# The context's second pointwise product of a convolution module in plain fp32, from unsplit maps and weights, with a third slot for raw weights

## The chip, the cores and the metric

The kernel runs on one NeuronCore of a Trainium2 chip, as one program. The metric is the device time of one execution in microseconds (us), smaller is better. It has five engines that are programmed apart and meet through semaphores: TensorE (PE, matrix products, with its weight loads shown as PEld), VectorE (DVE), ScalarE (ACT), GpSimd (POOL) and SyncE (SP, which here only issues transfers).

## The reference, cut to what matters

A backbone of two layers works on 1024 latent tokens and a context of 256 tokens, with 1024 features, all in fp32. Layer 0 is a Conformer convolution module, layer 1 grouped-query attention; a SwiGLU feed-forward follows each. The change lies in layer 0, in the two lines behind the convolution, for the context's tokens alone:

```python
def layernorm(x, g, b):
    mu = jnp.mean(xf, axis=-1, keepdims=True)
    var = jnp.mean(jnp.square(xf - mu), axis=-1, keepdims=True)
    y = (xf - mu) * lax.rsqrt(var + EPS)
    return (y * g + b)

def conv_module(h, w_pw1, b_pw1, w_dw, b_dw, ln_g, ln_b, w_pw2, b_pw2):
    u = h @ w_pw1 + b_pw1
    a, gt = jnp.split(u, 2, axis=-1)
    u = a * jax.nn.sigmoid(gt)
    u = lax.conv_general_dilated(u, w_dw, ...) + b_dw
    u = jax.nn.silu(layernorm(u, ln_g, ln_b))
    return u @ w_pw2 + b_pw2
```

Both streams, latent and context, go through it with the same weights.

## The kernel before, in words

Features lie on the 128 partitions, in 8 groups (KT), tokens along the free dimension. The tokens come in three pieces: C (the context, 256 tokens), L and R (the two halves of the latent tokens, 512 each).

**Products.** A large fp32 product is made of three fp32r products. An operand x is split into hi, its rounding to fp32r (a cast on ACT), and lo = x - hi (a subtraction on DVE); then hi\*hi, hi\*lo and lo\*hi are added up in one PSUM bank (`mm3`, L165 to L167; `mm3s`, L176 to L178, does the same for several weights at once, interleaved). `wload` (L135) brings a weight of 128x1024: SP loads it into a raw slot (tile `wr`, L141), ACT casts it (L142), DVE subtracts (L146). There are two raw slots and three buffers each for the halves (`wh`, `wl`). Weights that were loaded ahead wait in the list `self.pre`. Small products (sums over partitions with a column of ones, L363, transposes, L375, and the layer norm's mean, L562) take their operands in plain fp32, unsplit.

**The stage.** After the convolution, whose last maps DVE builds (L500) while PE uses them (L526 to L529), each piece goes through `ln` and `pw2`. `ln`: the mean over features (`mean`, L556: one fp32 product per phase of the tokens, 8 for C, 4 for L and for R, from the sums `vsum` that DVE made in the convolution); 8 times subtract it (DVE, L580), square (ACT), add up (DVE, L387); the sums of squares to a reciprocal root (`stat`: L363 on PE, small DVE steps L368 and L329 to L337, transposes L375 on PE); 8 times multiply (DVE, L588), Silu (ACT, L590) and split into the two halves (ACT L154, DVE L157). `pw2`: for each of 8 output groups a weight, 24 products (L603), bias and copy to SBUF (ACT, L604), square (ACT) and add (DVE, L387).

**The order of the work.** The program is written piece by piece: `ln` of C and of L, `pw2` of C, `ln` of R, `pw2` of L, post-norm of C and L, `pw2` of R, then the feed-forward. A scheduler in the framework reorders this by priority and data before it is fixed, so that on each engine the instructions of several pieces interleave; in the run each engine takes its own list strictly in order. So the mean of L and the mean of R stand on PE inside the products of C. A mean takes a PSUM bank of the pair 5 and 6 ("st"), which the transposed statistic of the piece before also uses and DVE reads in L588.

The names of tiles: `KB` holds C's convolution output and later its result, `T1` C's two halves, `T4` and `T2`, `T3` belong to L, `T5` and `T6`, `HS` to R; `q` is a room of 128x1024 that holds the convolution's split taps until the last maps are built; `HR` holds `vsum`; `vc` and `vl` are scratch in DRAM through which the convolution's output changes its layout.

Of the kernel before, what the change touches and what calls it, by code (L numbers as in the profile page):

```python
# [11 lines left out]
AF = mybir.ActivationFunctionType  # L12
ALU = mybir.AluOpType
AX = mybir.AxisListType

P = 128
D = 1024
KT = D // P
CTX = 256
# [17 lines left out]
PH = 8  # L37
# [17 lines left out]
class Kern:  # L55
# [79 lines left out]
    def wload(self, ap):  # L135
        nc = self.nc
        n = int(np.prod(ap.shape[1:]))
        raw = self.raw()[:, :n]
        hi = self.wp.tile([P, 1024], F32R, tag="wh", name="wh")[:, :n]
        lo = self.wp.tile([P, 1024], F32R, tag="wl", name="wl")[:, :n]  # L140
        nc.sync.dma_start(raw if len(ap.shape) == 2 else raw.rearrange("p (a b) -> p a b", a=ap.shape[1]), ap)  # L141
        nc.scalar.copy(hi, raw)  # L142
        self.share += self.lo_dve
        if self.share >= 1:
            self.share -= 1
            nc.vector.tensor_tensor(lo, raw, hi.bitcast(F32), op=ALU.subtract)  # L146
        else:
            nc.gpsimd.tensor_tensor(lo, raw, hi.bitcast(F32), op=ALU.subtract)
        return hi, lo

    def split(self, hi, lo, src, hi_eng="act"):
        nc = self.nc
# [403 lines left out]
    def mean(self, b):  # L556

        nc = self.nc
        ps = self.bank("st")
        nn, o, s0 = {"C": (NC_, 0, 0), "L": (NL, 2 + NC_, 0), "R": (NL, 2 + NC_, 4)}[b]  # L560
        for i in range(PH if b == "C" else 4):
            nc.tensor.matmul(ps[:, i * nn:(i + 1) * nn], lhsT=self.c["selp"][:, s0 + i:s0 + i + 1].to_broadcast([P, P]),  # L562
                             rhs=self.vsum[:, o:o + nn], start=True, stop=True)
        return ps
# [6 lines left out]
    def ln(self, b, stags, box):  # L571

        nc, c = self.nc, self.c
        c0, c1 = PIECES[b]
        n = c1 - c0
        cv = self.cvs[b]
        mean = self.mean(b)[:, :n]
        acc = self.acc(n)
        for k in range(KT):
            nc.vector.tensor_tensor(cv[:, k, :], cv[:, k, :], mean, op=ALU.subtract)  # L580
            self.sq_acc(acc, cv[:, k, :], k)
            yield
        pb = self.stat(acc, n)
        shi, slo = self.halves(*stags, n)
        box.append((shi, slo))
        for k in range(KT):
            z = cv[:, k, :]
            nc.vector.scalar_tensor_tensor(out=z, in0=z, scalar=c["lng"][:, k:k + 1], in1=pb,  # L588
                                           op0=ALU.mult, op1=ALU.mult)
            nc.scalar.activation(z, z, AF.Silu, bias=c["lnb"][:, k:k + 1], scale=1.0)  # L590
            self.split(shi[:, k, :], slo[:, k, :], z)
            yield

    def pw2(self, b, ytag, s, box):
# [4 lines left out]
        yacc = self.acc(n)  # L599
        box.append((y, yacc))  # L600
        for k in range(KT):
            o = self.bank("mm")
            self.proj(o, self.a["pw2"][k], self.pairs(*s), n)  # L603
            nc.scalar.activation(y[:, k, :], o[:, :n], AF.Identity, bias=c["bpw2"][:, k:k + 1], scale=1.0)  # L604
            self.sq_acc(yacc, y[:, k, :], k)
            yield 24 * n / 2400
# [338 lines left out]
    def build(self):  # L945
# [92 lines left out]
            self.split_u(KT - 1, g0, g0 + CG // 2)  # L1038
        self.derive(0, (1, 2))
        for i, _ in enumerate(cg):  # L1040
            if i in (2, 4):
                self.pre.append(self.wload(a["pw2"][i // 2 - 1]))
        self.set_banks(mm=[0, 1, 2, 3, 4, 7], st=[5, 6])
        sv, yv, fv = ({b: [] for b in PIECES} for _ in range(3))
        tags = {"C": ("KB", ("T1", "T1"), ("T1", "T1")), "L": ("T4", ("T2", "T3"), ("T2", "T3")),
# [11 lines left out]
            pass  # L1057
        for _ in self.pw2("L", tags["L"][0], sv["L"][0], yv["L"]):
            pass
        for b in ("C", "L"):  # L1060
            for _ in pp(b):
                pass
# [270 lines left out]
```

## Time and profile before

| | |
|---|---|
| Time, median of 3 runs | 3055.4 us (3049.22 to 3057.86) |
| Time of the profiled execution | 3058.17 us, 2.8 above that median |
| Span of the profiled execution, first to last instruction | 3056.4 us |
| Mean granted clock of TensorE | 0.974 |
| PE busy | 2927.2 us (96%) |
| DVE busy | 1902.2 us (62%) |
| ACT busy | 1207.4 us (40%) |

The profile is one execution, recorded instruction by instruction. In a row of the timeline stand the start in us, the duration (of a row with several instructions: of all of them), the engine, the line of the kernel, the operation, what it writes and reads, the shape and how many; in brackets how long the engine had been idle before, and what ended that. Records of matmuls overlap, since they are pipelined: what one costs is read from the distance of starts. The clock is the share of full speed granted to TensorE.

### The profile page before, as it was taken

The page shows a single profiled execution, that of the slowest core. Times are in us where ns is not written, and L with a number is a line of the kernel's source. Part 1 is how long each engine was busy: PE and PEld are TensorE (multiplying, and loading weights), DVE is VectorE, ACT ScalarE, POOL GpSimd, SP SyncE. Part 2 cuts the span into 40 slices and gives each one's busy share as a digit, 9 for nine tenths or more (in the row PEclk, how much of TensorE's full clock was granted, in tenths as well). Part 3 has the DMA queues.
Part 4 walks back from the last instruction along what each step waited for, and adds up shares of the span by engine and source line. Part 5 has one row for each costly group of instructions (what it writes and reads, how often), then busy time and mean ns, then how long its engine had stood idle before and what let it go on. Part 6 is the DMA issues. An engine that isn't in the chain of part 4 may idle for free. (4 is left out here: it accounts for less than half of the span.)

```text
span 3056.4 us, 39302 instructions
## 1 busy us (share of the span) xinstructions
PE 2927.2 (96%) x15086; PEld 2438.8 (80%) x15086; DVE 1902.2 (62%) x3341; ACT 1207.4 (40%) x1981; POOL 261.1 (9%) x413
## 2 busy tenths in 40 slices
PE   7899969999999999999988999999999999999997
PEld 5788868888888888888877777777787778788886
DVE  5886777866566358333565899766666654743335
ACT  5222255432222234222333688645555542332222
POOL 0000000101112011000013111110000000100000
PEclk9999979999999999999989999989999999999999
DMA  6542424433346235333346311223223132443332
GB/s 236 147 122 75 122 76 138 159 114 126 119 156 198 67 105 157 105 97 97 126 134 151 88 45 47 92 70 90 72 69 86 58 135 95 148 136 97 97 93 66
DMA packets 140716, 336.96 MB, mean 110 GB/s; under 512 B 39920, under 2 KB 61424, under 8 KB 139376
## 3 DMA queue, kind: packets, MB, share of 16 engines
q1 hardware_dynamic: 76432, 221.94, 22.6%
q0 software_dynamic: 37984, 104.42, 11.5%
q10 hardware_dynamic: 26112, 8.10, 1.1%
q8 instruction: 118, 1.93, 0.3%
q14 instruction: 70, 0.57, 0.1%
HBM read 289.76 MB, written 39.19 MB: 108 GB/s over the span
## 5 line engine op out<-in xcount | busy, mean ns | idle before, releaser
L167 PE MATMUL ps<-T,wl 128*128 128x512 f32 (+1 forms) x2128 | 802.9, 378 | 11.8 <-DVE wl L146 11.8
L165 PE MATMUL ps<-T,wh 128*128 128x512 f32 (+1 forms) x2128 | 806.3, 380 | 6.9 <-ACT T L154 4.1
L166 PE MATMUL ps<-T,wh 128*128 128x512 f32 (+1 forms) x2064 | 777.9, 377 | 0.7 <-DVE T L157 0.7
L142 ACT CAST wh<-wr 128x1024 fp32r<-128x1024 f32 x296 | 310.8, 1050 | 796.8 <-PE ps L166 569.0
L146 DVE TENSOR_TENSOR wl<-wr,wh 128x1024 fp32r<-128x1024 f32 x288 | 352.0, 1223 | 311.5 <-ACT wh L142 307.1
L167 PEld LDWEIGHTS ps<-T,wl 128*128 128x128 f32 x2128 | 407.3, 192 | 85.9 <-DVE wl L146 14.1
L165 PEld LDWEIGHTS ps<-T,wh 128*128 128x128 f32 x2128 | 407.2, 192 | 79.7 <-ACT T L154 5.6
L166 PEld LDWEIGHTS ps<-T,wh 128*128 128x128 f32 x2064 | 395.5, 192 | 68.9 <-DVE T L157 2.0
L166 PE MATMUL ps<-HS,wh 128*128 128x512 f32 (+1 forms) x784 | 303.8, 388 | 0.0
L892 DVE TENSOR_TENSOR T<-ps,T 128x512 fp32r<-128x512 f32 x320 | 216.7, 686 | 110.9 <-ACT T L891 109.7
L167 PE MATMUL ps<-HS,wl 128*128 128x512 f32 (+1 forms) x720 | 278.9, 388 | 0.0
L165 PE MATMUL ps<-HS,wh 128*128 128x512 f32 (+1 forms) x720 | 278.7, 389 | 0.0
L891 ACT CAST T<-ps 128x512 fp32r<-128x512 f32 x320 | 185.9, 585 | 194.8 <-PE ps L888 172.8
L888 PE MATMUL ps<-cst,T 128*128 128x128 f32 x1100 | 192.2, 276 | 1.9 <-DVE T L892 1.8
L876 DVE TENSOR_SCALAR_CACHE_REDUCE T<-ps,rq 128x1280 f32<-128x1280 f32 x110 | 169.9, 1544 | 27.8 <-PE ps L870 23.0
L722 DVE TENSOR_TENSOR T<-ps,T 128x512 f32<-128x512 f32 (+1 forms) x168 | 110.3, 662 | 113.1 <-PE ps L167 112.2
L888 PEld LDWEIGHTS ps<-cst,T 128*128 128x128 f32 x1100 | 134.0, 142 | 49.0 <-DVE T L892 28.6
L878 ACT ACTIVATE T<-T,mn 128x1280 f32<-128x1280 f32 x110 | 150.4, 1367 | 57.1 <-DVE T L876 55.2
L166 PEld LDWEIGHTS ps<-HS,wh 128*128 128x128 f32 x784 | 147.5, 188 | 28.6 <-DVE HS L157 0.2
L697 DVE TENSOR_TENSOR sm<-sm,ps 128x256 f32<-128x256 f32 (+1 forms) x88 | 54.5, 619 | 181.4 <-PE ps L167 181.2
L870 PE MATMUL ps<-KB,q 128*128 128x512 f32 (+1 forms) x576 | 146.8, 374 | 14.2 <-DVE HS L876 9.9
L167 PEld LDWEIGHTS ps<-HS,wl 128*128 128x128 f32 x720 | 135.4, 188 | 27.0
(227 smaller groups left out, 4574.0 us busy)
## 6 DMA issues: line engine op xcount, KB each, us to landing
wr<-in_w SPq DMA_DIRECT2D x220, 512.0 KB, 3.5
q<-in_w SPq DMA_DIRECT2D x44, 512.0 KB, 3.5
wr<-in_pw SPq DMA_DIRECT2D x40, 512.0 KB, 3.6
HR<-in_wmodT POOLq DMA_DIRECT2D x56, 256.0 KB, 3.9
q<-in_wmodT POOLq DMA_DIRECT2D x56, 256.0 KB, 3.9
qsd<-T POOLq DMA_DIRECT2D x32, 256.0 KB, 10.7
q<-qsd POOLq DMA_DIRECT2D x32, 256.0 KB, 3.3
wr<-in_wo SPq DMA_DIRECT2D x16, 512.0 KB, 4.4
```

What stands on the lines that cost most here:

```text
L142: nc.scalar.copy(hi, raw)
L146: nc.vector.tensor_tensor(lo, raw, hi.bitcast(F32), op=ALU.subtract)
L165: nc.tensor.matmul(out[:, :n], lhsT=wh, rhs=xh, start=k == 0, stop=False)
L166: nc.tensor.matmul(out[:, :n], lhsT=wh, rhs=xl, start=False, stop=False)
L167: nc.tensor.matmul(out[:, :n], lhsT=wl, rhs=xh, start=False, stop=k == nk - 1)
L722: nc.vector.tensor_tensor(yd, out[:, :c1 - c0], yd, op=ALU.add)
L870: nc.tensor.matmul(sc[:, k0:k0 + w], lhsT=q[:, h, :], rhs=kt[:, p * TOK + k0:p * TOK + k0 + w], start=p == 0, stop=p == 1)
L876: nc.vector.tensor_scalar(out=pt, in0=sc, scalar1=rq[:, h:h + 1], scalar2=None, op0=ALU.mult, op1=ALU.min, accum_out=mn)
L878: nc.scalar.activation(pt, pt, AF.Exp, bias=mn, scale=-1.0, accum_out=sums[:, 0, h:h + 1])
L888: nc.tensor.transpose(tp[:, h * P:(h + 1) * P], Ps[h][:, j * P:(j + 1) * P], c["ident"])
L891: nc.scalar.copy(ph, tp)
L892: nc.vector.tensor_tensor(pl, tp, ph.bitcast(F32), op=ALU.subtract)
```

## The change

For the context, and for it alone, `pw2` multiplies plain fp32 operands: 64 products of 128x256 (8 outputs by 8 groups) in the place of 192 fp32r products.

- `ln` of C writes Silu's result straight into one fp32 tile in `T1`; the 8 casts and 8 subtractions of its operand are gone.
- `pw2` of C takes its weights as they are loaded (`load_raw`), with no cast and no subtraction. A slot is free again when the 8 products that read it are done. The three weights that were loaded and split during the convolution are two now, and raw.
- From the eighth step of the last convolution loop on, the room `q` is a third raw slot, until `pw2` of L is written.
- `pw2` of L and of R take their first two weights as an interleaved pair (`projs`).
- The mean of C is one product of 256 columns with a matrix of ones; DVE first spreads `vsum` over the phases with one multiplication (L568 of the new kernel, the product is L570).

```diff
+    def load_raw(self, ap):
+        raw = self.raw()
+        self.nc.sync.dma_start(raw, ap)
+        return raw
...
-        nn, o, s0 = {"C": (NC_, 0, 0), "L": (NL, 2 + NC_, 0), "R": (NL, 2 + NC_, 4)}[b]
-        for i in range(PH if b == "C" else 4):
+        if b == "C":
+            m = self.sm(CTX)
+            mv, shape = m.rearrange("p (s n) -> p s n", n=NC_), [P, PH, NC_]
+            nc.vector.tensor_tensor(mv, self.vsum[:, :NC_].unsqueeze(1).to_broadcast(shape),
+                                    self.c["selp"].unsqueeze(2).to_broadcast(shape), op=ALU.mult)
+            nc.tensor.matmul(ps[:, :CTX], lhsT=self.c["ones"].to_broadcast([P, P]), rhs=m, start=True, stop=True)
+            return ps
+        nn, o, s0 = {"L": (NL, 2 + NC_, 0), "R": (NL, 2 + NC_, 4)}[b]
+        for i in range(4):
...
-        shi, slo = self.halves(*stags, n)
-        box.append((shi, slo))
+        if b == "C":
+            s = self.T(stags[0], [P, KT, n])
+            box.append(s)
+        else:
+            shi, slo = self.halves(*stags, n)
+            box.append((shi, slo))
...
+            if b == "C":
+                nc.scalar.activation(s[:, k, :], z, AF.Silu, bias=c["lnb"][:, k:k + 1], scale=1.0)
+                yield
+                continue
...
-            o = self.bank("mm")
-            self.proj(o, self.a["pw2"][k], self.pairs(*s), n)
+            if b == "C":
+                raw = self.pre.pop(0) if self.pre else self.load_raw(self.a["pw2"][k])
+                o = self.bank("mm")
+                for i in range(KT):
+                    nc.tensor.matmul(o[:, :n], lhsT=raw[:, i * P:(i + 1) * P], rhs=s[:, i, :], start=i == 0, stop=i == KT - 1)
+            else:
+                if k == 0:
+                    os = [self.bank("mm") for _ in range(2)]
+                    self.projs(os, self.a["pw2"][0:2], self.pairs(*s), n)
+                o = os[k] if k < 2 else self.bank("mm")
+                if k > 1:
+                    self.proj(o, self.a["pw2"][k], self.pairs(*s), n)
...
         for i, _ in enumerate(cg):
+            if i == 7:
+                self.raws.append(self.room())
             if i in (2, 4):
-                self.pre.append(self.wload(a["pw2"][i // 2 - 1]))
+                self.pre.append(self.load_raw(a["pw2"][i // 2 - 1]))
...
         for _ in self.pw2("L", tags["L"][0], sv["L"][0], yv["L"]):
             pass
+        self.raws.pop()
```

How it moves instructions is shown at three places. The first is PE where the mean of R stands (L562 before, L574 now, four products that read `HR`). Before, it was inside C's last products (they read T_3214, the halves in `T1`), with products of C behind it:

```order
L167 MATMUL ps<-T_3214,wl 128x256
L165 MATMUL ps<-T_3214,wh 128x256
L166 MATMUL ps<-T_3214,wh 128x256
L562 MATMUL ps<-HR,cst 128x128 x4
L167 MATMUL ps<-T_3214,wl 128x256
L165 MATMUL ps<-T_3214,wh 128x256
L166 MATMUL ps<-T_3214,wh 128x256
```

Now the products of C (L626) read the slots `wr_74`, `wr_73` and `q` one after the other; L368 and L380 are the statistic of L and its transposes, L181 to L183 the first products of L's pair:

```order
L626 MATMUL ps<-T_3202,wr_74 128x256 x8
L626 MATMUL ps<-T_3202,q 128x256 x2
L368 MATMUL ps<-cst,acc 128x1 x4
L626 MATMUL ps<-T_3202,q 128x256 x6
L380 MATMUL ps<-cst,nr 128x128 x4
L626 MATMUL ps<-T_3202,wr_73 128x256 x8
L626 MATMUL ps<-T_3202,wr_74 128x256 x8
L626 MATMUL ps<-T_3202,q 128x256 x8
L626 MATMUL ps<-T_3202,wr_73 128x256 x8
L574 MATMUL ps<-HR,cst 128x128 x4
L181 MATMUL ps<-T_3279,wh 128x512
L182 MATMUL ps<-T_3280,wh 128x512
```

The mean of R moved behind the last product of C and stands directly ahead of L's.

The second place is SP's queue of transfers at the end of the convolution. Before (`T_3014` and `T_3022` are `T4` and `T5`; `in_pw` are the weights):

```order
L141 DMA wr_74<-in_pw 128x1024
L569 DMA KB<-vc_89 128x256
L569 DMA T_3014<-vl_97 128x512
L569 DMA T_3022<-vl_97 128x512
L569 DMA T_3014<-vl_98 128x512
L569 DMA T_3022<-vl_98 128x512
L141 DMA wr_73<-in_pw 128x1024
```

Now (L153 is `load_raw`, L141 `wload`, which is L's from here on):

```order
L581 DMA T_3018<-vl_97 128x512
L153 DMA q<-in_pw 128x1024
L581 DMA T_3010<-vl_98 128x512
L581 DMA T_3018<-vl_98 128x512
L153 DMA wr_74<-in_pw 128x1024
L153 DMA wr_73<-in_pw 128x1024
L153 DMA wr_74<-in_pw 128x1024
L153 DMA q<-in_pw 128x1024
L153 DMA wr_73<-in_pw 128x1024
L141 DMA wr_74<-in_pw 128x1024
L141 DMA q<-in_pw 128x1024
```

The first load into `q`, C's fourth weight, goes ahead of the last two loads of the convolution's output; C's third weight, into `wr_74`, stands behind them.

The third place is DVE near the end of the convolution (L500, now L505, builds maps; L457, now L462, makes u for the last gather). Before:

```order
L500 TENSOR_TENSOR T_2697<-q,cst 128x640
L146 TENSOR_TENSOR wl<-wr_73,wh 128x1024
L500 TENSOR_TENSOR T_2697<-q,cst 128x640
L532 TENSOR_TENSOR HR<-HR,ps 128x162
L500 TENSOR_TENSOR T_2697<-q,cst 128x640
L552 TENSOR_REDUCE sm<-HR 128x162
L554 TENSOR_TENSOR HR<-HR,sm 128x162
L146 TENSOR_TENSOR wl<-wr_74,wh 128x1024
L457 SCALAR_TENSOR_TENSOR HR<-ps,cst,sm 128x512
```

Now:

```order
L505 TENSOR_TENSOR T_2697<-q,cst 128x640 x2
L537 TENSOR_TENSOR HR<-HR,ps 128x162
L505 TENSOR_TENSOR T_2697<-q,cst 128x640
L557 TENSOR_REDUCE sm<-HR 128x162
L559 TENSOR_TENSOR HR<-HR,sm 128x162
L462 SCALAR_TENSOR_TENSOR HR<-ps,cst,sm 128x512
```

The two subtractions that split weights of the second pointwise product are gone from between the maps, and nothing took their place.

## The prediction

> **What bounds the kernel now.** I read the page first: its engine totals, then its slices.
>
> ```profile
> span 3056.4 us, 39302 instructions
> PE 2927.2 (96%) x15086; PEld 2438.8 (80%) x15086; DVE 1902.2 (62%) x3341; ACT 1207.4 (40%) x1981; POOL 261.1 (9%) x413
> ...
> PE   7899969999999999999988999999999999999997
> ...
> PEclk9999979999999999999989999989999999999999
> ```
>
> TensorE (PE) is busy 96% of the span, so time is won only where it waits or runs at a low clock. Slice 6 (382 to 458 us) is the one with 6 tenths busy and clock 0.7. It holds the end of the convolution, the layer norms and the context's second pointwise product, where the change is. Next the windows of that stretch (columns: us, busy us of PE, PEld, DVE, ACT, POOL, then granted clock) and the timeline of PE.
>
> ```profile
> 400.00:410.00 10.00, 1.70 (x6) 1.22 (x6) 7.56 (x29) 4.61 (x11) 0.00 (x0) 0.50 0.09 34
> ...
> 440.00:460.00 20.00, 10.91 (x59) 9.75 (x60) 17.73 (x28) 15.38 (x28) 3.01 (x4) 0.70 0.30 105
> ```
>
> ```profile
> 395.87 2.91 PE L562 MATMUL ps<-HR,cst 128*128 128x32 f32 x16 [2.65 <-DVE HR L554]
> ...
> 410.27 1.01 PE L165 MATMUL ps<-T,wh 128*128 128x256 f32 x3 [1.81 <-ACT T L154]
> ...
> 420.92 0.28 PE L165 MATMUL ps<-T,wh 128*128 128x256 f32 x1
> ...
> 423.44 0.28 PE L165 MATMUL ps<-T,wh 128*128 128x256 f32 x1
> ...
> 424.47 0.39 PE L165 MATMUL ps<-T,wh 128*128 128x256 f32 x1 [0.64 <-ACT wh L142]
> ...
> 426.08 0.39 PE L167 MATMUL ps<-T,wl 128*128 128x256 f32 x1 [1.10 <-DVE wl L146]
> ...
> 445.52 2.08 PE L562 MATMUL ps<-HR,cst 128*128 128x128 f32 x8 [6.42 <-DVE T L588]
> ...
> 459.66 0.80 PE L167 MATMUL ps<-T,wl 128*128 128x512 f32 x1 [2.47 <-DVE wl L146]
> ...
> 473.66 0.39 PE L165 MATMUL ps<-T,wh 128*128 128x512 f32 x1
> ...
> 496.11 0.39 PE L165 MATMUL ps<-T,wh 128*128 128x512 f32 x1
> ...
> 506.31 0.50 PE L363 MATMUL ps<-cst,acc 128*128 128x1 f32 x4
> ```
>
> The context's product (C) starts at 410.27. Between 420.92 and 423.44 lie 21 matmuls, 0.12 us each, so its 192 need 23.0 us. Yet the last of them stand behind the mean of R, which came at 445.52. What fills the rest: waits for a weight's cast and subtraction (424, 426), the 6.4 us in which the mean of R, placed inside C's last products, waits for VectorE (DVE) to finish L's norm, and half clock behind each gap. Then the latent piece L begins, stops for a split weight, and runs from 459.66 to 506.31. Behind it 99 matmuls lie between 473.66 and 496.11: 0.227 us each, with no wait.
>
> **The change, part by part.** I keep the clock face of this execution and ask when L starts and ends.
>
> *Convolution's end.* Three of C's weights were split here. The last, in the timelines of ScalarE (ACT) and DVE:
>
> ```profile
> 360.93 1.05 ACT L142 CAST wh<-wr 128x1024 fp32r<-128x1024 f32 x1 [4.88 <-PE ps L449]
> ```
>
> ```profile
> 362.01 1.23 DVE L146 TENSOR_TENSOR wl<-wr,wh 128x1024 fp32r<-128x1024 f32 x1 [1.06 <-ACT wh L142]
> ...
> 398.82 1.41 DVE L580 TENSOR_TENSOR KB<-KB,ps 128x256 f32<-128x256 f32 x4 [3.00 <-PE ps L562]
> ...
> 408.50 2.83 DVE L588 SCALAR_TENSOR_TENSOR KB<-KB,cst,ps 128x256 f32<-128x256 f32 x7 [0.78 <-PE ps L375]
> ...
> 417.88 1.27 DVE L580 TENSOR_TENSOR T<-T,ps 128x512 f32<-128x512 f32 x2
> ...
> 436.89 2.06 DVE L588 SCALAR_TENSOR_TENSOR T<-T,cst,ps 128x512 f32<-128x512 f32 x3
> ```
>
> Behind 362 DVE builds the last maps for PE. At most the wait and the subtraction go, 1.06 + 1.23 = 2.3 us; at least nothing, if PE or the gather of u is late anyway. I take half, 1.2.
>
> *Mean of C.* Before, 2.95 us from 395.87 to DVE's first subtraction at 398.82. After: one DVE multiply (0.4, as one of L588's seven), then one product of 256 columns, 0.45 to 0.91 by the prices below, and 0.4 between engines: at most 1.75. It saves 1.2, between 1.2 and 1.7.
>
> *Price of an fp32 product of 128x256.* No such product is in the trace. The nearest:
>
> ```profile
> 57.74 1.91 PE L238 MATMUL ps<-T,cs 128*2 128x128 f32 x16
> 59.49 1.91 PE L238 MATMUL ps<-KB,cs 128*2 128x128 f32 x16
> ```
>
> ```profile
> L562 PE MATMUL ps<-HR,cst x32: 276/408/582, 395.9 to 447.2; 128*128 128x32 f32 x16, 128*128 128x128 f32 x16
> ```
>
> ```profile
> 55.00:63.00 8.00, 8.00 (x66) 6.13 (x64) 5.47 (x14) 5.20 (x18) 0.20 (x3) 1.00 0.07 17
> ```
>
> An fp32 matmul leaves two records (8 + 4 + 4 at L562 leave 32). At clock 1.00, 16 records of 128 columns took 59.49 - 57.74 = 1.75 us, 0.109 each, twice what one column per cycle would take. So 256 columns cost two records of 0.219, or of 0.227 if each goes like the 512-column fp32r rows. I take 0.454 per matmul, 29.1 for all 64, with 28.0 as the low end. **PE's own work grows by 6 us**, and the whole gain must come from waits. At half clock:
>
> ```profile
> 413.39 1.91 PE L562 MATMUL ps<-HR,cst 128*128 128x128 f32 x8
> 414.95 0.56 PE L165 MATMUL ps<-T,wh 128*128 128x256 f32 x1
> ...
> 468.62 0.95 PE L363 MATMUL ps<-cst,acc 128*128 128x1 f32 x8
> 469.43 0.49 PE L167 MATMUL ps<-T,wl 128*128 128x512 f32 x1
> ```
>
> Four matmuls of 128 columns took 1.56 us, 0.39 each; so 0.78 to 0.91 for 256, and I take 0.85. The L363 rows have one column, so they show the fp32 weight load nearly alone: 0.81 / 8 = 0.10 us. I count it as hidden under 0.227.
>
> Here a rule of the Trainium skill speaks against the change: "TensorE: Matmul & The Clock Gate", section "Measured speedup vs the span model", lets a weight load overlap a running matmul only when the two use different row groups, which full 128-row operands never do. By that rule the load would be paid each time (the second rival). The trace disagrees: L562's records at 413.39, with 128 columns and a load each, came 0.195 apart at half clock, while 0.109 and 0.10 in turn would be 0.21 even at full clock.
>
> *When the clock rises.* Two restarts, with clock by window:
>
> ```profile
> 415.00:418.50 3.50, 3.50 (x23) 3.50 (x22) 3.17 (x8) 1.26 (x2) 0.00 (x0) 0.69 0.00 0
> ...
> 445.00:451.50 6.50, 5.72 (x25) 5.42 (x26) 6.50 (x10) 4.21 (x8) 3.01 (x4) 0.52 0.40 127
> ```
>
> A mean of 0.69 is half clock for 2 x 0.31 x 3.5 = 2.2 us, to 417.2: 6.9 us after the restart at 410.27. A mean of 0.52 is half for 2 x 0.48 x 6.5 = 6.2, to 451.2: 5.7 us after the one at 445.52. I take 6.2.
>
> *C's product.* Silu now writes the operand itself:
>
> ```profile
> 409.02 0.91 ACT L590 ACTIVATE KB<-KB,cst 128x256 f32<-128x256 f32 x2 [4.32 <-DVE KB L588]
> ```
>
> One is out at 409.5, less 1.2 from the mean: PE starts at 408.3. Three matmuls (2.5), then the mean of L, 1.7 (it needs L588 done, 8 x 0.4 from 407.3 = 410.5: in time). Full clock at 414.5, by when 5.3 of 64 are done. The other 58.7 x 0.454 = 26.6. The products of L's statistic lie between, 0.8 as at 468.62, and its transposes, for which I put half of that. One wait for data: k=2's load goes into the first slot once k=0 is done, and a load takes 3.4 us
>
> ```profile
> wr<-in_pw SPq DMA_DIRECT2D x11, 512.0 KB, 3.4
> ```
>
> against 8 x 0.454 = 3.6 of k=1 that hide it; I put 0.5. If that cover is gone (a late load), up to 3.4 once. Later loads have two products of cover. SyncE's queue puts the third slot's load ahead of the last two vl loads. It waits for the last maps, they for the convolution's last output, which comes after those maps: it hides there. The mean of R follows C's last product, 0.9, and waits for nobody:
>
> ```profile
> 469.61 0.16 DVE L368 TENSOR_SCALAR nv<-ps 128x4 f32<-128x4 f32 x1
> ...
> 473.16 3.38 DVE L588 SCALAR_TENSOR_TENSOR T<-T,cst,ps 128x512 f32<-128x512 f32 x5 [1.21 <-PE ps L375]
> ```
>
> L's norm on DVE starts at 412.8 and takes 16 x 0.6 to 422.4; PE reaches its statistic behind 26 products, at 424.4, and 0.8 later DVE's small steps begin, 3.5 us as here; from 428.7 eight L588 and eight splits at no more than 0.69 end before 440. PE is the later one. Sum: 414.5 + 26.6 + 0.8 + 0.4 + 0.5 + 0.9 = **443.7**, where L starts.
>
> *Next late thing.* L's first two weights go as a pair. The second comes into q when C's k=6 is done (439.2), lands at 442.7, and 1.05 + 1.22 later is split, 445.0. The pair needs its low half at its seventh matmul, 443.7 + 6 x 0.227 = 445.1. Covered, with nothing over: each us later is a us lost.
>
> *L.* 192 x 0.227 = 43.6, R's statistics 1.2, and 1.0 because DVE has the split of L's fifth weight ahead of them, whose buffer only the end of the pair frees: L ends at 489.5, against 506.3. **16.8 us earlier**, and 1.2 from the convolution: 18.0. Taking C's 8 casts, 8 subtractions and 16 half-size splits off ACT and DVE gives nothing more beyond that.
>
> *Behind it.* C's statistic, the pieces' post-norms and the feed-forward start follow from 506.31 on the same engines with the same work, so the shift should be kept. The profiled execution took 3058.17 (1.8 outside its span); it becomes 3040.2. It lies 2.8 above the median of the runs, and the same 18.0 taken from that gives 3055.4 - 18.0 = **3037.4**.
>
> **Rivals.**
> *Clock stays at half through C's product* (it ends slower). Against it: clock 1.00 in the stretch of L238 rows, fp32 as well. For it: none of those has 128 weight columns. Each of 58.7 matmuls costs 0.40 more, 23.5; and L begins at half, 6 us that do the work of 3. 18.0 - 26.5 = -8.5: 3064. It decides from 45 of the 58.7 at half. Chance 0.04.
> *Weight loads are paid.* 128 x 0.10 = 12.8 less: 3050. Against: the 0.195 above. Chance 0.06.
> *The shift is lost where the feed-forward starts.* There ACT waits for loads and PE for the normed L:
>
> ```profile
> 561.36 1.05 ACT L142 CAST wh<-wr 128x1024 fp32r<-128x1024 f32 x1 [5.72 <-DMA wr<-in_w]
> ```
>
> ```profile
> 565.14 0.50 PE L176 MATMUL ps<-T,wh 128*128 128x512 f32 x1 [2.19 <-ACT T L400]
> ```
>
> Those loads wait for slots that DVE frees, and DVE follows C's statistic, so they should move too. If transfers collide anew and twice those 5.7 us come on top of today's wait, 11 go: 3048. If less, 3044. Chance 0.07, of which 0.04 under 0.3%.
> *The third slot does not feed C.* Two loads come late, 3.4 each: 3044. Chance 0.05.
>
> **How the numbers follow.** The forecast has 0.78. 0.3% is 9.2 us, about what a measurement of this kernel tells from no change. Faster by more: 0.78 + 0.05 + 0.03 = 0.86. Within: 0.06 + 0.04 = 0.10. Slower: 0.04. Low end: the other 1.1 of the convolution, 1.1 from the 28.0, 0.5 of the mean, and some 4 by which the runs of before spread: 3030. High end: convolution 0, one more late load, the rival at the feed-forward: 3047.
>
> **What would show it.** Right: L626 records at 0.22 to 0.23, PE without a gap over 1 us from 409 to 490, clock 1.00 from about 415, C's statistic 17 to 19 us earlier. Wrong: records at 0.3 or more, clock 0.5 behind 420, PE waiting for wr or q in C's product, or an early C's statistic with the first 512-column feed-forward product still near 565.

## The result: 18 us less, and where they went

The changed kernel took 3032.8 us (median of 6 runs, 3028.1 to 3034.4) against 3050.8 us for the kernel before in the same measurement (6 runs, 3047.4 to 3057.9). The ratio is 0.9936, with a 95% interval of 0.9922 to 0.9950. The difference of the medians, 18.0 us, is the sum that was predicted. That it agrees to the tenth is luck: the interval of the ratio leaves room for 15 to 24 us. The predicted time, 3037.4, came out 4.6 too high, because it was counted from the median of three runs, and the kernel before has a median that is 4.6 lower with six.

The two profiled executions differ by more, 23.7 us of span. The one of before was slower than its median of six by 7.4 us, the one of after by 1.6 (3034.4 against 3032.8). The difference of these, 5.7, is chance of the two executions.

First the page of the changed kernel: span, engine totals, and the slices of PE and its clock.

```profile
span 3032.7 us, 39111 instructions
...
PE 2919.0 (96%) x15008; PEld 2427.8 (80%) x15008; DVE 1892.2 (62%) x3326; ACT 1198.5 (40%) x1965; POOL 261.1 (9%) x413
...
PE   7999979999999999999988999999999999999997
...
PEclk9999989999999999999988999989999999999999
```

Slice 6, which had 6 tenths busy at clock 0.7, has now 7 tenths at 0.8. The windows of the stretch (us, busy of PE, PEld, DVE, ACT, POOL, granted clock) say what is left of its half clock:

```profile
400.00:410.00 10.00, 4.25 (x12) 3.32 (x13) 7.15 (x27) 5.22 (x11) 0.00 (x0) 0.50 0.01 2
410.00:420.00 10.00, 10.00 (x49) 8.83 (x49) 8.14 (x14) 6.39 (x13) 0.00 (x0) 0.94 0.31 107
420.00:440.00 20.00, 20.00 (x103) 17.64 (x102) 16.83 (x38) 14.70 (x29) 0.00 (x0) 1.00 0.40 133
```

PE is busy without a break from 410 on, at full clock behind 411.2 (a mean of 0.94 in 10 us is half clock for 1.2). Now the timeline of PE, from the context's product (L626) on:

```profile
407.45 2.93 PE L626 MATMUL ps<-T,wr 128*128 128x256 f32 x6 [1.12 <-ACT T L607]
410.17 1.54 PE L574 MATMUL ps<-HR,cst 128*128 128x128 f32 x8
411.55 9.23 PE L626 MATMUL ps<-T,wr 128*128 128x256 f32 x42
420.62 1.03 PE L626 MATMUL ps<-T,q 128*128 128x256 f32 x4
...
425.44 7.07 PE L626 MATMUL ps<-T,wr 128*128 128x256 f32 x32
432.35 3.62 PE L626 MATMUL ps<-T,q 128*128 128x256 f32 x16
435.81 3.62 PE L626 MATMUL ps<-T,wr 128*128 128x256 f32 x16
439.26 1.05 PE L574 MATMUL ps<-HR,cst 128*128 128x128 f32 x8
440.07 0.48 PE L181 MATMUL ps<-T,wh 128*128 128x512 f32 x1
...
485.61 0.50 PE L368 MATMUL ps<-cst,acc 128*128 128x1 f32 x4
...
486.29 0.40 PE L182 MATMUL ps<-HS,wh 128*128 128x512 f32 x1
...
530.75 0.51 PE L172 MATMUL ps<-T,wl 128*128 128x512 f32 x1 [1.98 <-DVE wl L146]
...
544.29 0.50 PE L181 MATMUL ps<-T,wh 128*128 128x512 f32 x1 [1.01 <-ACT T L405]
```

A row with brackets is one that waited. Behind 407.45 the next is at 530.75; before, four that the prediction quotes stood between 424 and 460 alone. The 32 records from 425.44 lie 0.216 us apart (6.91 / 32), so one fp32 product of 128x256, two records, takes 0.432 us. The mean of R comes behind the context's last product and waits for nobody; L starts at 440.07, and C's statistic stands at 485.61 instead of 506.31.

To compare the kernels of the experiments I use two counts. **To R** goes from the end of the last addition to `vsum` on DVE (the convolution's end) to R's first product that reads `HS`; **R to F** from there to a statistic of eight records inside the feed-forward. These are the ends of the counts before, DVE first:

```profile
395.49 0.33 DVE L554 TENSOR_TENSOR HR<-HR,sm 128x162 f32<-128x162 f32 x1
```

```profile
506.99 0.40 PE L166 MATMUL ps<-HS,wh 128*128 128x512 f32 x1
...
605.23 0.95 PE L363 MATMUL ps<-cst,acc 128*128 128x1 f32 x8
```

To R is 506.99 - 395.82 = 111.2 us, R to F 98.2. And in the changed kernel, with F at 583.63:

```profile
394.58 0.33 DVE L559 TENSOR_TENSOR HR<-HR,sm 128x162 f32<-128x162 f32 x1
...
396.68 1.42 DVE L592 TENSOR_TENSOR KB<-KB,ps 128x256 f32<-128x256 f32 x4 [1.31 <-PE ps L570]
...
440.44 1.23 DVE L146 TENSOR_TENSOR wl<-q,wh 128x1024 fp32r<-128x1024 f32 x1 [0.51 <-ACT wh L142]
```

To R is 486.29 - 394.91 = 91.4, R to F 97.3. So 19.8 us come from the stage that the change is about, 0.9 from R to F, and 0.9 of the two executions' difference lie ahead of the convolution's end, 2.1 behind F; nothing of the shift is lost at the feed-forward's start.

Where the 19.8 come from can be added up. C's first product starts 1.9 us sooner after the convolution's end. From there to R's first product it takes 96.7 us before (410.27 to 506.99) and 78.8 now (407.45 to 486.29). I cut both stretches into windows of a quarter of a us and add up PE's idle time, and for its busy time the share that the granted clock lacks. Before, PE idles 12.2 us and loses 12.0 to half clock; now it idles 0.0 and loses 1.9. What is left, the work at full clock, grows from 72.5 to 77.0 us. So **the waits give 12.2 us, the half clock 10.2, and PE's dearer products take 4.5 back**: almost half of what was won is clock.

### The profile page after: what moved, and what is told of

Its sections match the earlier page's. It is cut to its first block, busy times and chain, and to the rows that moved or that the text cites. A ratio compares the mean times of both kernels' runs of the same rounds, so it can differ in the third digit from the quotient of the medians.

```text
span 3032.7 us, 39111 instructions
## 1 busy us (share of the span) xinstructions
PE 2919.0 (96%) x15008; PEld 2427.8 (80%) x15008; DVE 1892.2 (62%) x3326; ACT 1198.5 (40%) x1965; POOL 261.1 (9%) x413
## 5 line engine op out<-in xcount | busy, mean ns | idle before, releaser
L172 PE MATMUL ps<-T,wl 128*128 128x512 f32 (+1 forms) x2032 | 769.6, 379 | 8.6 <-DVE wl L146 8.6
L170 PE MATMUL ps<-T,wh 128*128 128x512 f32 (+1 forms) x2032 | 772.3, 380 | 3.6 <-ACT T L159 2.2
L171 PE MATMUL ps<-T,wh 128*128 128x512 f32 (+1 forms) x1984 | 750.2, 378 | 0.2 <-DVE T L162 0.2
L142 ACT CAST wh<-wr 128x1024 fp32r<-128x1024 f32 x285 | 299.2, 1050 | 774.8 <-PE ps L171 542.7
L146 DVE TENSOR_TENSOR wl<-wr,wh 128x1024 fp32r<-128x1024 f32 x277 | 338.9, 1224 | 298.4 <-ACT wh L142 294.5
L172 PEld LDWEIGHTS ps<-T,wl 128*128 128x128 f32 x2032 | 386.3, 190 | 80.2 <-DVE wl L146 9.9
L170 PEld LDWEIGHTS ps<-T,wh 128*128 128x128 f32 x2032 | 386.7, 190 | 73.6 <-ACT T L159 3.3
L171 PEld LDWEIGHTS ps<-T,wh 128*128 128x128 f32 x1984 | 377.6, 190 | 67.5 <-DVE T L162 1.2
L171 PE MATMUL ps<-HS,wh 128*128 128x512 f32 (+1 forms) x768 | 297.1, 387 | 0.0
L922 DVE TENSOR_TENSOR T<-ps,T 128x512 fp32r<-128x512 f32 x320 | 216.8, 687 | 110.1 <-ACT T L921 108.9
L170 PE MATMUL ps<-HS,wh 128*128 128x512 f32 (+1 forms) x720 | 278.7, 389 | 0.0
L906 DVE TENSOR_SCALAR_CACHE_REDUCE T<-ps,rq 128x1280 f32<-128x1280 f32 x110 | 170.0, 1545 | 27.6 <-PE ps L900 22.7
```

What stands on the lines that cost most here:

```text
L170: nc.tensor.matmul(out[:, :n], lhsT=wh, rhs=xh, start=k == 0, stop=False)
L171: nc.tensor.matmul(out[:, :n], lhsT=wh, rhs=xl, start=False, stop=False)
L172: nc.tensor.matmul(out[:, :n], lhsT=wl, rhs=xh, start=False, stop=k == nk - 1)
L906: nc.vector.tensor_scalar(out=pt, in0=sc, scalar1=rq[:, h:h + 1], scalar2=None, op0=ALU.mult, op1=ALU.min, accum_out=mn)
L922: nc.vector.tensor_tensor(pl, tp, ph.bitcast(F32), op=ALU.subtract)
```

## The experiments

Twelve kernels, each timed against the kernel before.

| kernel | ratio to before (95%) | to R, us | R to F, us |
|---|---|---|---|
| before | 1 | 111.2 | 98.2 |
| changed | 0.9936 (0.9922 to 0.9950) | 91.4 | 97.3 |
| no third slot | 0.9980 (0.9968 to 0.9992) | 99.1 | 99.8 |
| mean of C by eight products | 0.9960 (0.9945 to 0.9975) | 93.1 | 97.6 |
| third slot, mean, pairs; no fp32 | 1.0026 (1.0011 to 1.0041) | 114.0 | 101.3 |
| before, mean of R later | 1.0011 (1.0001 to 1.0021) | 110.1 | 98.1 |
| no pairs | 0.9937 (0.9919 to 0.9955) | 91.9 | 97.2 |
| L in fp32 too | 1.0014 (1.0003 to 1.0025) | 103.4 | 102.7 |
| third slot kept to the modulation | 0.9958 (0.9941 to 0.9974) | 91.8 | 93.6 |
| casts and subtractions put back | 1.0036 (1.0023 to 1.0049) | 113.5 | 103.7 |
| casts put back | 1.0025 (1.0011 to 1.0038) | 109.4 | 104.7 |
| subtractions put back | 1.0022 (1.0012 to 1.0033) | 114.6 | 102.3 |
| mean and pairs alone | 1.0027 (1.0014 to 1.0039) | 112.9 | 100.4 |
| third slot to the end of R's product | 0.9982 (0.9971 to 0.9993) | 92.1 | 109.4 |

One thing must be known before any of them is read: the framework's scheduler makes the order anew for every kernel. C's statistic stands on PE behind all 192 of L's products in the kernel before, in the changed one, and in those with eight mean products, without pairs, with R's mean later and with either of the last slots; and behind L's 64 where L is fp32 too. In the other six it stands inside L's product. And the feed-forward begins in another interleaving of its pieces in eight: those six, L in fp32, and the slot to the end of R's product (from R's first product to F there are 469 to 479 records of matmuls in every kernel, 477 in the one before). An edit that looks like one cost can so bring a second one with it, and it did.

**The parts that cost little: mean and pairs.** The changed kernel with the mean as it was (the branch for C taken out again):

```diff
-        if b == "C":
-            m = self.sm(CTX)
-            ...
-            nc.tensor.matmul(ps[:, :CTX], lhsT=self.c["ones"].to_broadcast([P, P]), rhs=m, start=True, stop=True)
-            return ps
-        nn, o, s0 = {"L": (NL, 2 + NC_, 0), "R": (NL, 2 + NC_, 4)}[b]
-        for i in range(4):
+        nn, o, s0 = {"C": (NC_, 0, 0), "L": (NL, 2 + NC_, 0), "R": (NL, 2 + NC_, 4)}[b]
+        for i in range(PH if b == "C" else 4):
```

> The changed kernel with the mean of C by 8 products again. Theory: the mean stands on the chain from the convolution's last sum to C's first product, nothing beside it, so the 1.2 us come back: stage 91.9 (90.7 with the one product), time within the noise. Rival (the chain has slack): 90.7.

Its DVE row at the place where the changed kernel has 396.68 (the convolution ended at 396.35 here):

```profile
399.85 0.42 DVE L585 TENSOR_TENSOR KB<-KB,ps 128x256 f32<-128x256 f32 x1 [3.50 <-PE ps L567]
```

From the convolution's end to DVE's first subtraction it takes 3.5 us, with the one product 1.77. To R is 1.7 us longer, and nothing else changes. The ratio stands 0.0024 above the changed kernel's (some 7 us), but the two intervals overlap; the 1.7 is what the traces show.

The changed kernel without the pairs:

```diff
-                if k == 0:
-                    os = [self.bank("mm") for _ in range(2)]
-                    self.projs(os, self.a["pw2"][0:2], self.pairs(*s), n)
-                o = os[k] if k < 2 else self.bank("mm")
-                if k > 1:
-                    self.proj(o, self.a["pw2"][k], self.pairs(*s), n)
+                o = self.bank("mm")
+                self.proj(o, self.a["pw2"][k], self.pairs(*s), n)
```

> The changed kernel with L's and R's first two weights one after the other and not as a pair. Theory: L's operand is complete when TensorE reaches L, so interleaving by feature group hides nothing; without it the second weight is needed 5.4 us later and the 0.2 us of wait go: stage 90 to 91. Rival (the pair covers L's norm): stage 92 or more.

Ratio 0.9937 against 0.9936, to R 91.9 against 91.4: the pairs are worth nothing that shows.

**fp32 and the third slot, each without the other.** First the changed kernel without the slot:

```diff
-            if i == 7:
-                self.raws.append(self.room())
...
-        self.raws.pop()
```

> The changed kernel without the third raw slot. The stage is measured from the end of the last sum of the convolution on VectorE to C's first statistic behind L's product: 110.5 us before, 90.7 after. My theory: a slot is free only when its 8 products are done, so with two slots C's loads have 3.46 us of cover against 3.4 to 3.5 us of transfer (some tenths of a wait per weight), and L's second weight can be fetched only when C's last product is over: some 3.5 + 2.3 us behind it, of which the pair needs it after 1.4 and the mean of R hides 0.9. Stage 95 to 97, time 4 to 6 us over the changed kernel. Rival, the third slot hides nothing that two would not: stage within 0.7 of 90.7.

It lost 0.0044, about 13 us, two to three times the 4 to 6 that were expected. PE's rows:

```profile
410.32 2.92 PE L626 MATMUL ps<-T,wr 128*128 128x256 f32 x6 [1.11 <-ACT T L607]
...
428.28 14.28 PE L626 MATMUL ps<-T,wr 128*128 128x256 f32 x64
442.40 1.05 PE L574 MATMUL ps<-HR,cst 128*128 128x128 f32 x8
444.56 0.50 PE L181 MATMUL ps<-T,wh 128*128 128x512 f32 x1 [1.11 <-ACT wh L142]
...
453.96 0.50 PE L170 MATMUL ps<-T,wh 128*128 128x512 f32 x1 [2.38 <-ACT wh L142]
```

The context's product did not wait at all: from its first record to the mean of R it took 32.1 us, 31.8 with the third slot. Two slots feed it. What came late were L's first weights. SP's queue issued the first of them at 439.02 here (a row of 8 transfers to 480):

```profile
439.02 41.72 SPq L141 DMA_DIRECT2D wr<-in_pw  x8
```

and at 432.55 in the changed kernel, 7.5 us ahead of L's first product:

```profile
432.55 0.33 SPq L141 DMA_DIRECT2D wr<-in_pw  x1
```

So the third slot works for L, while C's product runs, and not for C. How much of the 13 us is that and how much the other order of the feed-forward (R to F 2.5 longer) is not separated; to R alone makes 7.8.

Then the kernel before with the slot, the one-product mean and the pairs, and the three fp32r products as they were (against the changed kernel; only the lines of the product are shown, the operand and the weights are split as before too):

```diff
-            if b == "C":
-                raw = self.pre.pop(0) if self.pre else self.load_raw(self.a["pw2"][k])
-                o = self.bank("mm")
-                for i in range(KT):
-                    nc.tensor.matmul(o[:, :n], lhsT=raw[:, i * P:(i + 1) * P], rhs=s[:, i, :], start=i == 0, stop=i == KT - 1)
+            if b == "C":
+                o = self.bank("mm")
+                self.proj(o, self.a["pw2"][k], self.pairs(*s), n)
```

> The kernel before with all of the change but fp32: third raw slot, mean of C by one product, pairs for L and R, and still three fp32r products from split maps and weights for C. My theory (the gain is TensorE no longer waiting for splits): the mean's 1.2 us and 1 to 4 from earlier loads, stage 105 to 108. Rival (slots, mean and the new order do it, fp32 is by the way): stage 91 to 96.

It is slower than before by 0.26%. The theory's figure missed, since 114.0 us to R are more than before and not 3 to 5 fewer. The waits that the prediction counted are all there, the one at the mean of R half as long:

```profile
422.12 0.39 PE L167 MATMUL ps<-T,wl 128*128 128x256 f32 x1 [1.10 <-DVE wl L146]
...
444.45 2.08 PE L569 MATMUL ps<-HR,cst 128*128 128x128 f32 x8 [3.06 <-DVE T L595]
...
458.50 0.80 PE L178 MATMUL ps<-T,wl 128*128 128x512 f32 x1 [2.87 <-DVE wl L146]
```

The mean of R stands behind C's last product here (two of L's products are ahead of it) and still waits 3.06 us: while C needs 8 weights cast and subtracted, DVE is not through with L's norm when PE is through with C.

To have all four corners, the mean and the pairs alone in the kernel before:

```diff
-            o = self.bank("mm")
-            self.proj(o, self.a["pw2"][k], self.pairs(*s), n)
+            if k == 0 and b != "C":
+                os = [self.bank("mm") for _ in range(2)]
+                self.projs(os, self.a["pw2"][0:2], self.pairs(*s), n)
...
+            m = self.sm(CTX)
+            ...
+            nc.tensor.matmul(ps[:, :CTX], lhsT=self.c["ones"].to_broadcast([P, P]), rhs=m, start=True, stop=True)
```

> The kernel before, with the context's mean by one product and the pairs of L's and R's first two weights, without fp32 and without the third slot. Theory (the mean is worth 1.2 to 1.9 us, the pairs nothing, and what made the version with a third slot but without fp32 lose 3 us up to R's first product is the slot): 109 to 110.5 us from the convolution's end to R's first product, time 1 to 2 us under before. Rival (the pairs lose where weights must be split): 113 or more, time 3 to 8 us over before.

The theory missed: not the slot, but these two edits, or one of them, with the new order make the loss, 1.0027 without the slot and 1.0026 with it. The rival's figures came nearer (112.9 us to R, some 8 us over before), but that the pairs are the cause is not shown. C's statistic moved into L's product, and the feed-forward got its other interleaving:

```profile
440.24 2.08 PE L569 MATMUL ps<-HR,cst 128*128 128x128 f32 x8 [6.18 <-DVE T L595]
...
550.85 0.80 PE L167 MATMUL ps<-T,wl 128*128 128x512 f32 x1 [4.38 <-DVE wl L146]
```

With mean and pairs in all four, the corners are 1.0027 with neither, 1.0026 with the slot, 0.9980 with fp32, 0.9936 with both. **The slot alone gives nothing, fp32 alone 0.0047 or some 14 us, and the slot on top of fp32 another 13.** That these sum to 28 and not to 18 is the 0.0027 that mean and pairs lose when they are put into the kernel before, and not with fp32 and slot together. Three of the four corners have the other order, so these are prices of the edits with their orders. The 14 us of fp32 alone are the fairest of them: both kernels of that pair have C's statistic inside L's product and the other interleaving of the feed-forward.

**Is the mean of R alone the culprit?** In the kernel before, its products were given a later priority:

```diff
-            nc.tensor.matmul(ps[:, i * nn:(i + 1) * nn], lhsT=..., rhs=..., start=True, stop=True)
+            with self.later(400 if b == "R" else 0):
+                nc.tensor.matmul(ps[:, i * nn:(i + 1) * nn], lhsT=..., rhs=..., start=True, stop=True)
```

> The kernel before with one thing: the four products of R's mean get a later place in the order, behind C's products, as they stand in the changed kernel. Theory: those last products of C wait for a weight's split that VectorE makes at the same time anyway, so the 6.4 us of wait change their name: stage 107 to 111 against 110.5. Rival (the place of the mean of R is the gain): stage 100 to 104.

The stretch to R, 110.1 us, is what the theory expected, but it says nothing: the four products kept their place among C's, so that the wait stayed too.

```profile
446.70 2.08 PE L563 MATMUL ps<-HR,cst 128*128 128x128 f32 x8 [7.10 <-DVE T L589]
```

What a kernel with split operands and a later mean of R would take is answered only by the row at 444.45 above: the mean still waits.

**L in fp32 too**, with the same edit for L as for C:

```diff
-        if b == "C":
+        if b != "R":
             s = self.T(stags[0], [P, KT, n])
...
-            if b == "C":
+            if b != "R":
                 raw = self.pre.pop(0) if self.pre else self.load_raw(self.a["pw2"][k])
```

> The changed kernel with L in fp32 too, 64 products of 128x512 from unsplit operands. Theory: L's stretch is bound by TensorE; 128 records of 1024 array cycles at the 0.216 us per 512 cycles of C's records give 55.3 us for the 43.7 of now, so stage 102 to 103 and time 10 to 12 us over the changed kernel. Rival (the splits that go free ScalarE and VectorE and pay for it): at most 5 over.

```profile
471.21 7.03 PE L626 MATMUL ps<-T,q 128*128 128x512 f32 x16
478.08 13.90 PE L626 MATMUL ps<-T,wr 128*128 128x512 f32 x32
...
527.55 0.65 PE L380 MATMUL ps<-cst,nr 128*128 128x128 f32 x4 [2.30 <-DVE sb L400]
...
544.23 0.79 PE L172 MATMUL ps<-T,wl 128*128 128x512 f32 x1 [3.75 <-DVE wl L146]
```

Records of 512 columns lie 6.87 / 16 = 0.429 us apart, so a product takes 0.859 against 3 x 0.227 = 0.681 for the three fp32r ones. For L's 64 that is 11.4 us, and to R is 12.0 longer, as expected. The time is not: 0.0078 above the changed kernel's ratio are 24 us, twice the 10 to 12 that were expected. The product in fp32 is dearer by a quarter on PE; it pays where PE waited for the splitting, as in C's product, and not in L's, which no longer waits. R to F, with the other interleaving, adds 5.4; the rest lies outside these two counts.

**Is it the work taken off ACT and DVE?** The changed kernel with C's weights cast and subtracted again, into halves that nobody reads:

```diff
         self.nc.sync.dma_start(raw, ap)
+        hi = self.wp.tile([P, 1024], F32R, tag="wh", name="wh")
+        lo = self.wp.tile([P, 1024], F32R, tag="wl", name="wl")
+        self.nc.scalar.copy(hi, raw)
+        self.nc.vector.tensor_tensor(lo, raw, hi.bitcast(F32), op=ALU.subtract)
         return raw
```

> The changed kernel in which C's weights are split again by ScalarE and VectorE, 8 casts of 1.05 us and 8 subtractions of 1.22, into halves that nobody reads; TensorE's products are the changed ones. It tells load from dependency. If the relief of VectorE is part of the gain: L's norm and the first split weights of L, which ended 0.2 us late for TensorE, come 5 to 7 us later, stage 95 to 98. Rival (only TensorE's dependence on the splits cost): stage within 1 of 90.7.

The loss was 22 us up to R, three to four times the 5 to 7 that were expected, and all of the gain. To see which engine it is, the casts alone and the subtractions alone (raw minus raw):

```diff
         self.nc.sync.dma_start(raw, ap)
+        hi = self.wp.tile([P, 1024], F32R, tag="wh", name="wh")
+        self.nc.scalar.copy(hi, raw)
         return raw
```

> The changed kernel, with each of the context's 8 weights also cast on ACT into a half that nobody reads; no subtraction on DVE. Counted from the end of the convolution to R's first product: before 111.2 us, changed 91.4, with both idle casts and idle subtractions 113.5. Theory (DVE is the engine that sets when L is ready; ACT has air): the 8 casts of 1.05 us cost little, 92 to 97, time 3034 to 3040. Rival (ACT sets it, since PE waited for casts of L's first weights when both were put back): 105 to 113, time 3050 to 3062.

```diff
         self.nc.sync.dma_start(raw, ap)
+        lo = self.wp.tile([P, 1024], F32R, tag="wl", name="wl")
+        self.nc.vector.tensor_tensor(lo, raw, raw, op=ALU.subtract)
         return raw
```

> The changed kernel, with a subtraction of 128x1024 on DVE for each of the context's 8 weights, into a half that nobody reads; no cast on ACT. Same count from the convolution's end to R's first product. Theory (DVE sets when L is ready): the 8 subtractions of 1.22 us and what queues behind them cost most of the 22 us that both together cost, 103 to 112, time 3046 to 3060. Rival (ACT sets it): 92 to 97, time 3034 to 3040.

Each alone costs nearly as much as both (109.4 and 114.6 against 113.5), so the two loads do not add up. By the figures, the casts alone fell into their rival's range (105 to 113), and the subtractions alone just beyond their theory's (103 to 112). But ACT and DVE cannot each be the one engine that sets the time. Look at the kernel with the casts, in which DVE has not one instruction more. The cast of L's first weight on ACT, its subtraction on DVE, and what waits on PE:

```profile
441.55 1.04 ACT L142 CAST wh<-wr 128x1024 fp32r<-128x1024 f32 x1
```

```profile
451.32 1.22 DVE L146 TENSOR_TENSOR wl<-wr,wh 128x1024 fp32r<-128x1024 f32 x1
```

```profile
444.88 0.50 PE L183 MATMUL ps<-T,wh 128*128 128x512 f32 x1 [1.50 <-ACT wh L142]
...
447.91 0.80 PE L172 MATMUL ps<-T,wh 128*128 128x512 f32 x1 [2.29 <-ACT wh L142]
...
452.59 0.79 PE L185 MATMUL ps<-T,wl 128*128 128x512 f32 x1 [3.46 <-DVE wl L146]
...
476.95 0.32 PE L382 MATMUL ps<-cst,nr 128*128 128x128 f32 x1 [3.50 <-DVE nr L344]
```

From C's first product to R's, PE idles 11.0 us here and 0.0 in the changed kernel. There are three kinds of wait. The first is for ACT's casts of L's weights, 4.0 us with one of 0.21 that is not shown. In part that is load: two idle casts, from 439.00 on, stand ahead of the cast at 441.55, which comes 44.7 us after the convolution's end, against 42.7 in the changed kernel. The second, 3.46, is the place in DVE's list. The cast is done at 442.6, but the subtraction starts at 451.3, because DVE works through R's norm first, which now stands ahead of it; in the changed kernel the same subtractions, the second of them at 440.44, stand ahead of R's norm. The third, 3.50, is the place in PE's list: C's statistic now stands inside L's product, and PE waits there for its small steps on DVE. The other two kernels have these waits too (6.4, 3.05 and 3.50 with both put back; 4.1, 4.09 and 3.50 with the subtractions), and in both DVE ends L's norm later, 48.2 and 49.0 us after the convolution's end against 41.9 in the changed kernel. That is load again.

So load and order both cost time in these runs, and neither theory nor rival names both. What the 8 casts or the 8 subtractions would cost with the order held is not shown. With them put back the kernel is no faster than with split products and the same slot, mean and pairs (1.0022 to 1.0036 against 1.0026). How much of fp32's gain is that PE no longer waits for C's splits, and how much that ACT and DVE are free for L's, therefore stays open.

**How long to keep the third slot.** Kept until the modulation needs the room, and until R's product is written:

```diff
-        self.raws.pop()
...
+            self.raws.pop()
             q = self.room()
```

> The changed kernel that keeps the third raw slot through R and into the feed-forward, until the modulation needs the room. Theory: where the feed-forward starts, ScalarE waits twice some 4.5 us for weights whose slot comes free late, and TensorE idles 2.0, 1.0 and 0.7 us; with three slots 2 to 4 us go: from C's statistic to the first 512-column product of the feed-forward 55 to 57 us, against 58.7. The stage stays at 90.7. Rival (VectorE's chain of post-norms sets that start): 58 to 59.

```diff
-        self.raws.pop()
...
         for _ in self.pw2("R", tags["R"][0], sv["R"][0], yv["R"]):
             pass
+        self.raws.pop()
```

> The changed kernel, with the third slot kept until R's product is written instead of L's. Theory (the waits that are left in the changed kernel, 1.98 us for the low half of a weight in R's product and 1.7 at the feed-forward's start, are waits for slots): R's product loses its wait, the time is 0 to 4 us under the changed kernel, 3029 to 3033. Rival (a longer third slot shifts the order and the waits move behind the feed-forward's start, as when it was kept still longer): 3036 to 3040.

The second loses clearly; for the first the ratio is 0.0022 above the changed kernel's, and the two intervals just overlap. Up to R both are as fast as the changed kernel. With the slot kept to the modulation the waits of 1.0 and 0.7 us at the feed-forward's start are gone, as the theory said (56.7 us from C's statistic to the feed-forward's first product of 512 columns), and F comes 3.7 us sooner after R; but later waits have come, and from F to the end it takes 2457.7 us against 2449.1 (3032.7 less 583.63) in the changed kernel:

```profile
591.94 0.50 PE L170 MATMUL ps<-T,wh 128*128 128x512 f32 x1 [1.59 <-ACT sm L726]
597.36 0.58 PE L172 MATMUL ps<-T,wl 128*128 128x256 f32 x1 [4.69 <-DVE wl L146]
```

With the slot to R's end the theory missed: the wait in R's product stayed, at 2.06 us. The difference that shows is the order of the feed-forward, and it costs 12.1 us from R to F. Its first weights, cast (two in the row), subtracted, and waited for:

```profile
533.02 1.99 ACT L142 CAST wh<-wr 128x1024 fp32r<-128x1024 f32 x2 [4.62 <-DMA wr<-in_w]
```

```profile
549.15 1.21 DVE L146 TENSOR_TENSOR wl<-wr,wh 128x1024 fp32r<-128x1024 f32 x1
```

```profile
550.42 0.58 PE L183 MATMUL ps<-T,wl 128*128 128x256 f32 x1 [9.54 <-DVE wl L146]
```

The first cast is done by 534.1, and 15 us pass to the subtraction, which DVE has queued behind a norm of 512 columns (L400 and L406, from 537.4 on). In the changed kernel DVE does a subtraction just ahead of that norm:

```profile
536.49 1.22 DVE L146 TENSOR_TENSOR wl<-wr,wh 128x1024 fp32r<-128x1024 f32 x1
```

None of the twelve is faster than the changed kernel.

## Why the prediction was right, point by point

*The sum.* Predicted 18.0, measured 18.0 between medians. By the traces the stage gave 19.8 against 16.8, and the convolution nothing against 1.2; the smaller steps missed in both directions:

- **Convolution's end, 1.2 us: wrong.** From the first `TENSOR_REDUCE` of the stretch to the convolution's end it takes 75.9 us before and 75.8 after. Over the fourteen profiles, the four whose products of C take split weights have 75.4 to 75.9, the others 75.8 to 77.2. The wait and the subtraction at 362 were hidden; the bound of nothing was the right one.
- **Mean of C, 1.2: right.** From the convolution's end to DVE's first subtraction it was 3.0 and is 1.77.
- **Price of an fp32 product: 0.454 taken, 0.432 measured**, just under the low end of 0.438 that the 0.109 per 128 columns gave. Over 58.7 products that is 1.3 us of the 3 that the stage gave beyond the sum. The fp32 weight load stays hidden. The rule of the Trainium skill that the prediction argued against, by which a weight load overlaps a running matmul only when their row groups differ, stands in "TensorE: Matmul & The Clock Gate" in the section "The mechanism", just ahead of the section that the prediction names. It does not hold for these records: 0.216 us at 256 columns leaves no room for the 0.10 that a load took nearly alone.
- **Clock up 6.2 us after the restart: too late for this execution, and the 1.2 us that it gave are chance.** It was 3.8 here (407.45 to 411.2), which is 1.2 us of work. Read in the same way, the other nine kernels with C in fp32, none of which waits in those first microseconds, give 3.1 to 5.9 us after C's first product: without the third slot 3.3 (410.32, and a mean of 0.67 from 407 to 417), with the subtractions put back 5.9 (408.35, and 0.64). The four with split operands, which wait some 0.45 us once more 1.5 us after their start, give 3.8 to 6.9. The 3.8 is that of the kernel with mean and pairs alone (start at 408.43, wait at 409.88, a mean of 0.74 from 407 to 417), so such a wait does not start the count anew there. What sets the moment is not shown. In these fourteen executions it varies by 3.8 us, and two profiles can differ by half of that through it alone. Of the 10.2 us of half clock above, some 1.6 are this (6.9 before, 3.8 now). The Trainium skill, in the same page's section "What's actually happening", puts the rise at about 3.4 us of sustained work, and says that it varies by 0.5 us with where in a free-running window the first matmul lands. The earliest rises here lie near the 3.4, but the spread is wider, 3.1 to 6.9.
- **A wait of 0.5 for k=2: did not come.** The 42 records from 411.55 run through at 0.216. With the clock and the price these make the 3.0: L was to start 47.9 us after the convolution's end, and started after 45.2 (440.07 - 394.91), and L itself took 0.3 less than predicted.
- **The mean of R waits for nobody: right**, 439.26 without a bracket.
- **L's second weight is covered, with nothing over: right.** Its subtraction ended at 441.67, and the pair's seventh product, due 6 x 0.227 after 440.07, at 441.4, had slipped by 0.3.
- **L: right.** From its start to C's statistic 45.5 us, predicted 45.8.
- **The shift is kept: right.** The first 512-column product of the feed-forward that waits went from 565.14 to 544.29.
- **"Taking the casts and subtractions off gives nothing more beyond that": open.** To put them back cost the whole gain, in part by their load and in part by another order.

*The rivals.* Half clock through C's product: refuted by 1.00 from 420 on. Paid weight loads: refuted by the 0.216. Shift lost at the feed-forward: not with the changed kernel's order, though the kernel with the slot to R's end shows that the danger was real, with a price of 12 us, but by an order of DVE's list, not by the collision of transfers that the prediction had in mind. Third slot not feeding C: it brings two of C's weights, but C does not need it; the prediction's reason for the slot was wrong, and the gain it gave by feeding L was in the sum without being priced.

## What to carry to other kernels

One dearer product can win where the cheaper ones need their operands prepared on engines that are on the path: compare PE's price (here 64 x 0.432 = 27.6 us for 23.0) with the waits for preparation in that stage and the half clock behind them, and stop where the waits stop, as L in fp32 shows. A spare buffer serves whoever is next in the queue of loads, so look for its worth at the next consumer. Where a scheduler remakes the order, compare the order of each engine's list before calling a difference the cost of an edit: the three experiments that were to add load also moved a subtraction behind a norm.

## What the runs showed of the hardware that was not expected

- An fp32 product goes at two records of 0.216 us for 256 columns and of 0.429 us for 512 at full clock, with its weight load hidden; three fp32r products of 512 columns take 0.681 together and one fp32 product 0.859.
- The clock rose 3.1 to 5.9 us after the start of C's fp32 product in ten kernels in which it ran without a wait, and 3.8 to 6.9 us after the start of the split product in four kernels that waited 0.45 us once more 1.5 us in. Starts that look alike in the list of instructions so had full clock up to 2.8 us sooner or later.
